# Low halves made on chip, a sixth pair, one power per norm and paced loads of x in a hybrid layer kernel

## The chip, the core and the metric

The kernel runs on one core of a Trainium2 chip, as one launch. The metric is the device time of that launch in microseconds; several runs are taken and their median is compared. The profile is of one execution more, recorded by the hardware profiler. In it PE is the matmul engine (TensorE), PEld its weight load, DVE the vector engine, ACT the scalar engine, POOL is GpSimd and SP the engine that only issues transfers.

## What is computed

One layer over 2048 prompt tokens and 64 tokens of a separate sample, which carries its own convolution history and its own state. Cut to what matters:

```python
h = rms_norm(x, g_pre)
vA, bA, cA, zA, q, f, iv, zB, gA, gB = split(h @ w_in)            # ten blocks of 1024 columns
conv = causal_conv3(concat(conv_hist, cA * vA), conv_w)
yA = (silu(zA) * bA * conv) @ w_a_out                              # convolution path
fg = lb + (1 - lb) * sigmoid(f); logf = log(fg); kk = 1 - fg       # attention path, 8 heads of 128
for each chunk of 64 tokens, b = cumsum(logf), ref = b[middle]:
    att = tril((qq * exp(b - ref)) @ (kk * exp(ref - b)).T)
    o = att @ vv + (qq * exp(b)) @ S
    S = exp(b_last) * S + (kk * exp(b_last - b)).T @ vv
o = o * rsqrt(mean(o * o) + 1e-6) * g_onorm
yB = (o * silu(zB)) @ w_b_out
x = x + rms_norm((sigmoid(gA) * yA + sigmoid(gB) * yB) @ w_o, g_post)
x = x + (p @ w_ple_proj) * sigmoid(rms_norm(x, g_ple) @ w_ple_gate)
```

The sample goes through the same layer with its own history and state.

## The kernel before

**Blocks.** Prompt and sample are laid in one row of 2112 tokens, the sample at place 1408. It is worked off in three blocks of 768, 704 and 640 tokens (`plan`, from L47). Everything is kept with features on the 128 partitions and tokens along the free dimension. The first block has six pairs of 64-token chunks, the second five pairs of the prompt and the sample's lone 64-token chunk, the third five pairs.

**Large products.** A float32 product is made of three matmuls in fp32r: high weight by high input (L442), high weight by low input (L443), low weight by high input (L444). `sgroup` makes two output blocks of 128 features at once by a scheme of seven products in place of eight, over halves of the contraction and of the tokens: its weight blocks are `A11`, `S3`, `S1`, `S2`, `A12`, `A22`, `S4`, in this order; `A..` are weights as they are, `S..` are sums of them. Each product takes 4 x 3 matmuls. `in_turn` (L593 to L595) and `gemm` (L631 to L633) do the same for the later products.

**Weights.** In the first block `combined` loads four weight blocks, makes the sums, and `split_w` makes of each block a high half on ACT and a low half on DVE (both recorded at L226, in `split`); the low halves and the sums are stored to HBM through SP for the later blocks (L280, L331), where `used_later` says so. In the later blocks `kept_w` loads the block (L236), ACT casts the high half (L273) and SP loads the stored low half (L274). Weight tiles rotate: five raw ones, four high ones, four plus three low ones (`lo` and `s` by turns, `low_tile`).

**Order.** Path B of a block (`path_b`) goes over eight heads. A head takes two groups by `sgroup` (f with iv, then zB with q). After each of the seven products `hook()` runs one prepared step, so the small float32 matmuls of a head's attention (`head_attn`) are put between the products of the groups that follow. In a block that is not the first the steps of one head stand at fixed slots: 2 (first part's scores), 3 (second part's), 6 (updates of the state, all pairs), 8 (outputs), 11 (`turn_o`), 14 (`read_o`), 21 (`scale_o`); the sample's chunk, a part of its own, has steps at 4 (two transposes and scores), 5 (update), 7 (output) and 10 (transpose back). The keys, values and outputs of the pairs are turned from features to tokens without PE: DVE transposes in 32 x 32 blocks (L1054), POOL stores to HBM (`turned`, L1056) and loads back in another order (`in_rows`, L1061); the keys are then copied by POOL (L1066) to the tile that the state updates read (L1126). Path A (`path_a`) follows with sixteen groups of `sgroup` (vA with cA, zA with bA), then the products with `w_a_out`, `w_b_out`, `w_o`. In the second block `prepare_sums` makes on the side, in path A, the sums for `w_b_out` for the block that follows.

**Norms.** At a block's end `final_norm` is spread by hooks over the next block's gate products. `col_rstd` sums squares over features by transposes (L709), a reduction (L711), a scaling (L686) and a power on POOL (L689), once for each half of the block; `rms` puts the result on all partitions by transposes again (`spread`, L700). x is loaded for it on POOL's queue (L1423), four tiles of 128 features ahead.

Of the kernel before, what the change touches and what calls it, by code (L numbers as in the profile page):

```python
# [47 lines left out]
def plan():  # L48
# [3 lines left out]
    for size in SIZES:  # L52
# [8 lines left out]
        assert all(g["len"] == 2 * CH for g in groups[:npair])  # L61
        parts = [groups[i : min(i + 4, npair)] for i in range(0, npair, 4)] + [[g] for g in groups[npair:]]
        halves = [dict(t0=t0 + o, off=o, n=size // 2) for o in (0, size // 2)]
        out.append(dict(t0=t0, n=size, runs=runs, npair=npair, parts=parts, groups=groups, segs=halves, last=t0 + size == TOK))
# [29 lines left out]
def hybrid_step(  # L94
# [102 lines left out]
    lone = [const.tile([P, 1, P], F32, tag=f"lone{i}", name=f"lone{i}") for i in range(3)]  # L197

    def constants():
        for rows, odd, base in ((slice(0, P), 0, 0), (slice(0, CH), 1, -CH), (slice(CH, P), 1, CH)):  # L200
            tri = rt(P)
            G.memset(tri, 1.0)
            G.affine_select(
                out=tri, in_=tri, pattern=[[1, P]], compare_op=ALU.is_ge, fill=0.0, base=base, channel_multiplier=-1
            )
            V.tensor_copy(caus[odd][rows], tri[rows])
        V.memset(keep, 1.0)
        V.memset(keep.rearrange("p (c t) -> p c t", t=CH)[:, :, 0:1], 0.0)
        for t in atts + lone:
            V.memset(t, 0.0)  # L210
# [40 lines left out]
    def used_later(idx, part):  # L251
# [5 lines left out]
        if idx in (GB * 8 + KB - 1, IV * 8):  # L257
            return part != 0
        if W_B <= idx < W_O:
# [74 lines left out]
    def kept_w(i1, i2, name, anew=False, spread=False):  # L334

        keys = dict(A11=(i1, 0), A12=(i1, 1), A22=(i2, 1))
        if name in keys:
            return split_w(load_raw(w_blk[keys[name]]), None if anew else keys[name], spread)
# [346 lines left out]
    def rstd_of(ms_ap, out_ap, scale, start=0):  # L685
# [3 lines left out]
        powers[:] = [G.tensor_tensor(out_ap, out_ap, mhalf[start : start + shape[0], :].to_broadcast(shape), ALU.pow).ins]  # L689
        return scaled  # L690

    def cols_tile(n):
        return small.tile([P, (n + P - 1) // P], F32, tag="cols", name=nm("cols"))
# [9 lines left out]
    def col_rstd(acc, n):  # L703

        pc = ps_attn()
        cols = cols_tile(n)
        with placed():
            for i, o in tiles_of(n):
                T.transpose(pc[:, i * P : i * P + P], acc[:, o : o + P], ident)  # L709
        count = cols.shape[1]  # L710
        V.tensor_reduce(cols, pc[:, : count * P].rearrange("p (i c) -> p i c", c=P), axis=mybir.AxisListType.X, op=ALU.add)  # L711
        rstd_of(cols, cols, 1.0 / D)
        return cols

    def rms(acc, out, segs, hasten=False):


        cols = [col_rstd(acc[:, cols_of(sg)], sg["n"]) for sg in segs]
# [217 lines left out]
    def head_prep(bl, hc, hd, first, hs, before):  # L936
        n, npair = bl["n"], bl["npair"]
        nch, np1 = n // CH, npair * P
        sf, vt = rt(), rt()

        def sink_f(c, h, x, y):
# [9 lines left out]
            into(half(vt, h)[:, n1:], x[:, n1:], None if y is None else y[:, n1:])  # L951
# [5 lines left out]
        lg, b, eq, qx = rt(), rt(), rt(), rt()  # L957
        wrote = [turned("tv", vt, qx, npair)]
# [8 lines left out]
        ka, kb, qe, z = hf(npair * CH), rt(), rt(), rt()  # L967

        def scaled(after):
# [17 lines left out]
            more = npair - 2 * SWAP  # L987
            for lo, hi, to in (
                (0, SWAP, ka3[:, more + 1 :: 2, :]),
                (SWAP, 2 * SWAP, ka3[:, more : npair - 1 : 2, :]),  # L990
                (2 * SWAP, npair, ka3[:, :more, :]),
            ):
                own = slice(2 * lo, 2 * hi, 2)
                V.tensor_tensor(to, chunks(sf)[:, own, :], chunks(lg)[:, own, :], ALU.mult)
                scale = f2[:, lo:hi].unsqueeze(2).to_broadcast([P, hi - lo, CH])
                place = slice(2 * lo + (hi <= SWAP), 2 * hi, 2)
                V.tensor_tensor(chunks(kb)[:, place, :], to, scale, ALU.mult)
# [3 lines left out]
            if not first:  # L1001
                wrote.append(turned("tk", kb, b, npair))
            if nch % 2:
                end = slice(nch - 1, nch)
                V.tensor_tensor(chunks(kb)[:, end, :], chunks(sf)[:, end, :], chunks(lg)[:, end, :], ALU.mult)
# [28 lines left out]
        with behind_all([*wrote, *powers]):  # L1034
            by_token = [in_rows("tv", npair)]
            if before is not None and not first:
                before["ot"] = in_rows("to", npair, before["on"])
            if not first:
                by_token.insert(0, in_rows("tk", npair))
        return dict(  # L1040
            eq=eq, f=f, ka=ka, kb=kb, qe=qe, qx=qx, vt=vt, z=z, by_token=by_token, on=None,
            npair=npair, more=npair - 2 * SWAP, first=first, last=bl["last"], carry=None,
# [26 lines left out]
    def head_attn(ip, gs, d, hd):  # L1069
# [3 lines left out]
        nt, ln = len(gs), gs[0]["len"]  # L1073
        o0, n = gs[0]["off"], nt * ln
        qe, z, att = d["qe"], d["z"], atts[ip]
        single = ln < P
        assert (nt == 2 * SWAP) == (o0 == 0)
        rows = slice(P - ln, P)

        def tile3(i=None):  # L1080
            if single and i is not None:
                return lone[i]
            if nt == 1:
                return small.tile([P, 1, P], F32, tag="one", name=nm("one"), bufs=5)
            return cols3(rt(nt * P), nt)

        def cols(t, g):
            end = g["off"] + ln
# [4 lines left out]
        ready = [] if single else [t[:, o0 // P : o0 // P + nt] for t in d["by_token"]]  # L1093
        for q, src in enumerate((d["kb"], d["vt"])[: 2 - len(ready)]):
            turn_ = ps_attn()
            with placed():
                for i, g in enumerate(gs):
                    T.transpose(turn_[:, i * P : i * P + P], cols(src, g), ident)
            ready.insert(q, tile3(q))
            A.copy(ready[q][rows], cols3(turn_, nt)[rows])  # L1100
        kt, v = ready
        p_a = ps_attn()
        with placed():
            for i, g in enumerate(gs):
                o = g["off"]
                shared = nt == 2 * SWAP
                if not single and (i < SWAP or not shared):
# [4 lines left out]
                T.matmul(p_a[:, i * P + CH : i * P + P], cols(d["kb"], g), qe[:, o + ln - CH : o + ln], start=True, stop=True)  # L1112
        pa3 = cols3(p_a, nt)

        if single:
            V.copy_predicated(att[CH:, :nt, CH:], caus[0][CH:, CH:].unsqueeze(1).to_broadcast([CH, nt, CH]), pa3[CH:, :, CH:])
        else:
            for swapped, lo, hi in ((1, 0, SWAP), (0, SWAP, nt)) if nt == 2 * SWAP else ((0, 0, nt),):
                mask = caus[swapped].unsqueeze(1).to_broadcast([P, hi - lo, P])
                V.copy_predicated(att[:, lo:hi], mask, pa3[:, lo:hi])  # L1120
# [8 lines left out]
        sample = gs[0]["sample"]  # L1129
        if sample:  # L1130
            cur = small.tile([P, P], F32, tag="s0", name=nm("s0"), bufs=1)
            G.dma_start(cur, s0[hd])
        else:
            cur = states[hd] if d["carry"] is None else d["carry"]
        for i, g in enumerate(gs):
            u = p_u[:, i * P : i * P + P]
            c = (g["off"] + ln) // CH - 1
# [7 lines left out]
        if g["end"]:  # L1145
# [6 lines left out]
            if sample:  # L1152
# [5 lines left out]
        else:  # L1158
            d["carry"] = cur
# [9 lines left out]
        if not single:  # L1169
            d["on"] = rt(d["npair"] * P) if d["on"] is None else d["on"]  # L1170
            on = cols3(d["on"][:, o0:], nt)
        else:
            on = tile3(2)
        ms = small.tile([P, 4], F32, tag="ms", name=nm("ms"))
        po3 = cols3(p_o, nt)
        if d["first"]:
            for i in range(nt):
                A.activation(on[rows, i, :], po3[rows, i, :], AF.Square, accum_out=ms[rows, i : i + 1])
        else:
            A.activation(on[rows], po3[rows], AF.Square)  # L1180
            V.tensor_reduce(ms[rows, :nt], on[rows], axis=mybir.AxisListType.X, op=ALU.add)
        rstd_of(ms[rows, :nt], ms[rows, :nt], 1.0 / P, P - ln)
# [605 lines left out]
```

## Time and profile before

| | |
|---|---|
| median of 3 runs | 2545.3 us (2542.03 to 2548.34) |
| the profiled execution | 2544.89 us, of which the span 2543.2 us |
| DVE, ACT, POOL busy | 71%, 59%, 18% of the span |
| granted TensorE clock | 1.000 |
| 16 DMA engines | 67.0% of their time on SP's queue, 21.3% on POOL's; 781.01 MB |

PE is busy 99% of the time. A page with such a figure is read by what PE executes and by the few places where it stands: its instructions in order of time, and the view of waits cut down to PE. A float32 matmul appears as two records (x2), a transpose as one; a large product's matmul as one. "Mean ns" of a matmul is from its start to its modelled end and overlaps the next one, so the price of one is read from start to start.

### The profile page before, as it was taken

How to read it: one execution, taken by the hardware profiler on the slowest of the kernel's cores; microseconds unless marked ns; L12 is line 12 of the kernel's file. 1: busy time of each engine (PE TensorE's matmuls, PEld its weight loads, DVE VectorE, ACT ScalarE, POOL GpSimd, SP SyncE). 2: the span in 40 equal slices, each digit the busy share in tenths (PEclk: the TensorE clock that was granted, in tenths of full speed). 3: DMA queues.
4: the chain of work that ended last, by engine and by line, in shares of the span. 5: the costliest groups of instructions: out<-in, count | busy, mean ns of one | idle time of the engine just before them, and what ended most of it. 6: DMA issues, size and time to landing. Idle time of an engine off the chain costs nothing.

```text
span 2543.2 us, 46984 instructions
## 1 busy us (share of the span) xinstructions
PE 2524.2 (99%) x16022; PEld 2511.2 (99%) x16022; DVE 1796.8 (71%) x3533; ACT 1499.3 (59%) x2940; POOL 462.7 (18%) x809
## 2 busy tenths in 40 slices
PE   9999999999999999999999999999999999999998
PEld 9999999999999999999999999999999999999998
DVE  7889888889868775467774557988347755336967
ACT  6766676554453764466655556567456665446674
POOL 2012121221022022122221221102212221001011
PEclk9999999999999999999999999999999999999999
DMA  8789888999797888988889998989999999999985
GB/s 331 246 291 340 305 297 304 349 354 328 258 345 250 274 288 306 309 286 299 294 298 308 357 380 307 327 289 308 333 306 317 319 337 322 298 299 327 334 270 195
DMA packets 371937, 781.01 MB, mean 307 GB/s; under 512 B 45990, under 2 KB 50912, under 8 KB 371696
## 3 DMA queue, kind: packets, MB, share of 16 engines
q1 hardware_dynamic: 321840, 582.95, 67.0%
q0 software_dynamic: 49856, 195.04, 21.3%
q8 instruction: 126, 2.06, 0.3%
q14 instruction: 115, 0.94, 0.1%
HBM read 562.57 MB, written 215.24 MB: 306 GB/s over the span
## 4 chain that ended last, share of the span: by engine, by line
PE 89%; DMA 4%; issue 3%; DVE 2%; ACT 0%; POOL 0%; SPq 0%; DVEq 0%; POOLq 0%; ACTq 0%
PE pg L442 19%; PE pg L444 19%; PE pg L443 19%; PE pg L593 5%; PE pg L594 5%; PE pg L595 5%; PE pg L632 3%; PE pg L633 3%; PE pg L631 3%; PE pa L1126 1%; PE pa L1166 1%; DMA lo<-low 1%; PE pa L1168 1%; PE pa L1112 1%; DMA s<-low 1%
## 5 line engine op out<-in xcount | busy, mean ns | idle before, releaser
L442 PE MATMUL pg<-r,hi 128*128 128x320 f32 (+2 forms) x3304 | 1078.7, 326 | 0.1
L443 PE MATMUL pg<-r,hi 128*128 128x320 f32 (+2 forms) x3304 | 1067.8, 323 | 0.0
L444 PE MATMUL pg<-r,lo 128*128 128x384 f32 (+2 forms) x2368 | 772.5, 326 | 1.7 <-DMA lo<-low 1.5
L273 ACT CAST hi<-raw 128x512 fp32r<-128x512 f32 x726 | 447.2, 619 | 486.3 <-PE pg L443 188.1
L442 PEld LDWEIGHTS pg<-r,hi 128*128 128x128 f32 x3304 | 621.6, 188 | 0.8 <-ACT hi L226 0.4
L443 PEld LDWEIGHTS pg<-r,hi 128*128 128x128 f32 x3304 | 621.4, 188 | 0.0
L444 PEld LDWEIGHTS pg<-r,lo 128*128 128x128 f32 x2368 | 444.6, 188 | 2.8 <-DMA lo<-low 2.1
L444 PE MATMUL pg<-r,s 128*128 128x320 f32 (+1 forms) x936 | 295.8, 316 | 2.0 <-DMA s<-low 2.0
L594 PE MATMUL pg<-r,hi 128*128 128x320 f32 (+2 forms) x864 | 277.5, 322 | 0.0
L593 PE MATMUL pg<-r,hi 128*128 128x320 f32 (+2 forms) x864 | 274.9, 322 | 0.2 <-ACT r L226 0.2
L226 ACT CAST hi<-raw 128x512 fp32r<-128x512 f32 x252 | 155.4, 621 | 151.5 <-PE pg L443 41.3
L226 DVE TENSOR_TENSOR r<-r,r 128x320 fp32r<-128x320 f32 (+7 forms) x350 | 206.4, 609 | 43.9 <-ACT r L226 42.9
L226 ACT CAST r<-r 128x320 fp32r<-128x320 f32 (+7 forms) x350 | 183.3, 557 | 43.9 <-DVE r L390 9.3
L226 DVE TENSOR_TENSOR lo<-raw,hi 128x512 fp32r<-128x512 f32 x231 | 157.7, 687 | 71.8 <-ACT hi L226 67.8
L595 PE MATMUL pg<-r,lo 128*128 128x352 f32 (+2 forms) x564 | 180.8, 321 | 0.4 <-DMA lo<-low 0.4
L444 PEld LDWEIGHTS pg<-r,s 128*128 128x128 f32 x936 | 176.0, 188 | 2.6 <-DMA s<-low 2.6
L226 ACT CAST hi<-s 128x512 fp32r<-128x512 f32 x160 | 98.9, 620 | 130.1 <-PE pg L443 106.1
L632 PE MATMUL pg<-r,hi 128*128 128x384 f32 (+2 forms) x512 | 167.5, 328 | 0.2 <-DVE r L226 0.2
L631 PE MATMUL pg<-r,hi 128*128 128x384 f32 (+2 forms) x512 | 166.0, 328 | 0.5 <-ACT hi L226 0.3
L594 PEld LDWEIGHTS pg<-r,hi 128*128 128x128 f32 x864 | 162.1, 188 | 1.2 <-DVE r L226 0.8
L593 PEld LDWEIGHTS pg<-r,hi 128*128 128x128 f32 x864 | 161.3, 188 | 1.6 <-ACT r L226 1.2
L456 ACT COPY hf<-pg 128x352 f32<-128x352 f32 (+2 forms) x354 | 157.4, 447 | 1.2 <-PE pg L444 0.8
(393 smaller groups left out, 4134.9 us busy)
## 6 DMA issues: line engine op xcount, KB each, us to landing
raw<-w_blk SPq DMA_DIRECT2D x578, 256.0 KB, 4.5
raw<-S SPq DMA_DIRECT2D x440, 256.0 KB, 4.6
lo<-low SPq DMA_DIRECT2D x421, 256.0 KB, 4.4
s<-low SPq DMA_DIRECT2D x305, 256.0 KB, 4.5
low<-lo SPq DMA_DIRECT2D x275, 256.0 KB, 4.2
S<-s SPq DMA_DIRECT2D x156, 256.0 KB, 4.0
low<-r POOLq DMA_DIRECT2D x50, 256.0 KB, 5.9
r<-w_blk POOLq DMA_DIRECT2D x48, 256.0 KB, 7.3
```

What stands on the lines that cost most here:

```text
L226: return A.copy(hi, src).ins, V.tensor_tensor(lo, src, hi.bitcast(F32), ALU.subtract).ins
L273: A.copy(hi, raw)
L442: add(hi[:, k, :], xhi, start=start and k == 0, stop=False)
L443: add(hi[:, k, :], xlo, start=False, stop=False)
L444: last[0] = add(lo[:, k, :], xhi, start=False, stop=k == KH - 1).ins
L456: copied = A.copy(got[n], ps[bank])
L593: add(hi[:, k, :], xhi, start=start and k == 0, stop=False)
L594: add(hi[:, k, :], xlo, start=False, stop=False)
L595: last[0] = add(lo[:, k, :], xhi, start=False, stop=k == KH - 1).ins
L631: T.matmul(ps, hi[:, k % 4, :], xhi[:, c], start=k == ks[0], stop=False)
L632: T.matmul(ps, hi[:, k % 4, :], xlo[:, c], start=False, stop=False)
L633: last[0] = T.matmul(ps, lo[:, k % 4, :], xhi[:, c], start=False, stop=k == ks[-1]).ins
```

## The change

1. **Low halves.** In path A of the second and third block the low halves of `A12` and `A22` of the four weights vA, bA, cA, zA are made by DVE from the raw tile, as in the first block, in place of the load; the first block does not store them.
2. **Sixth pair.** The sample's chunk becomes the second half of a sixth pair, whose first half has zero values and a copy of the chunk's keys. It shares the part of the fifth pair: its keys, values and outputs go through the same transposes on DVE and the same way through HBM (now 768 columns wide in place of 640), its scores come out of the fifth pair's first matmul, its update and output stand in that part's steps. The steps at slots 4, 5, 7 and 10 go.
3. **One power.** `col_rstd` takes both halves of a block, and makes one scaling and one power of all columns. In the plan of hooks the spreading of a block's first norm comes one hook later; five idle hooks between the norms become four.
4. **x one by one.** In the first two blocks the four loads ahead become one at each of the four steps that sum squares, and each load of x is held behind the last matmul issued before it (`paced`).
5. `prepare_sums` in the second block's path A takes its steps at groups' turns 0, 1, 3, 5, 7 in place of 3 to 7.

```diff
@@ used_later
+        if idx < QQ * 8:
+            return part != 1
@@ kept_w
-            return split_w(load_raw(w_blk[keys[name]]), None if anew else keys[name], spread)
+            return split_w(load_raw(w_blk[keys[name]]), None if anew else keys[name], spread or keys[name][0] < QQ * 8 and keys[name][1] == 1)
@@ col_rstd
+        count = len(tiles_of(n))
+        cols = small.tile([P, 2 * count], F32, tag="cols", name=nm("cols"))[:, : len(accs) * count]
+        outs = [cols[:, q : q + count] for q in range(0, len(accs) * count, count)]
+        for acc, out in zip(accs, outs):
+            pc = ps_attn()
...
+            V.tensor_reduce(out, pc[:, : count * P].rearrange("p (i c) -> p i c", c=P), axis=mybir.AxisListType.X, op=ALU.add)
         rstd_of(cols, cols, 1.0 / D)
-        return cols
+        return outs
@@ head_prep
+        odd_end = turn > npair
+        sf, vt = rt(), rt(turn * P)
+        if odd_end:
+            V.memset(vt[:, n - CH : n], 0.0)
...
+            if odd_end:
+                V.tensor_copy(chunks(kb)[:, nch - 1 : nch + 1, :], ka3[:, more - 1 : more, :].to_broadcast([P, 2, CH]))
...
-                wrote.append(turned("tk", kb, b, npair))
-            if nch % 2:
-                end = slice(nch - 1, nch)
-                V.tensor_tensor(chunks(kb)[:, end, :], chunks(sf)[:, end, :], chunks(lg)[:, end, :], ALU.mult)
+                wrote.append(turned("tk", kb, staged_k, turn))
@@ head_attn
+                if mixed:
+                    if i == 0:
+                        c = o // CH
+                        to = p_a[:, : 2 * 3 * CH].rearrange("p (g c) -> p g c", c=3 * CH)[:, :, :CH]
+                        T.matmul(to, d["ka"][:, :P], chunks(qe)[:, c : c + 3 : 2, :], start=True, stop=True)
...
+        if mixed:
+            V.copy_predicated(att[CH:, nt - 1, CH:], caus[0][CH:, CH:], pa3[CH:, nt - 1, CH:])
...
-        yield
-        p_t = ps_attn()
-        with placed():
-            for i in range(nt):
-                T.transpose(p_t[:, i * P : i * P + P], on[:, i, :], ident)
-        c = slice(o0, o0 + n)
-        V.tensor_tensor(z[:, c], p_t[:, P - ln : P - ln + n], z[:, c], ALU.mult)
@@ path_b
-                pairs, one = attn[:2], attn[2:]
-                for slot, steps in enumerate((pairs[:1], pairs[1:], one, one, pairs, one, pairs, (), one)):
+                for slot, steps in enumerate((attn[:1], attn[1:], (), (), attn, (), attn)):
@@ final_norm
-                G.dma_start(xks[j][:, c], x_fm[j * P : (j + 1) * P, segs[0]["t0"] : segs[0]["t0"] + n])
-
-        for _ in range(2 if bl["last"] else 4):
+                load = G.dma_start(xks[j][:, c], x_fm[j * P : (j + 1) * P, segs[0]["t0"] : segs[0]["t0"] + n])
+                if not bl["last"]:
+                    paced(load)
+
+        if kept is None:
             fetch()
-        if kept is not None:
+            fetch()
+        else:
             for j in range(KB):
                 sum_squares(j, xo[j], acc, width[0])
                 if j % 2:
+                    fetch()
                     yield
@@ side
-                if j >= 3:
+                if j in (0, 1, 3, 5, 7):
                     next(sums_, None)
@@ the plan of the first two blocks' norms
-            spread_out((norm, (1, 1, 1, 1, 0, 0, 1, 0, 1) + (0, 1) * KB + (0, 0, 0, 0, 0, 1, 0, 1) + (0, 1) * KB))
+            spread_out((norm, (1, 1, 1, 1, 0, 0, 1, 0, 0, 1) + (0, 1) * KB + (0, 0, 0, 0, 1, 0, 1) + (0, 1) * KB))
```

157 lines of the change are left out of this document (74 added, 83 removed).

## The prediction

> **What bounds the kernel now.** I read the page's head and chain first, then the view of waits for PE alone (total, times, longest), then PE's instructions around each wait.
>
> ```profile
> span 2543.2 us, 46984 instructions
> ...
> PE 2524.2 (99%) x16022; PEld 2511.2 (99%) x16022; DVE 1796.8 (71%) x3533; ACT 1499.3 (59%) x2940; POOL 462.7 (18%) x809
> ...
> PE 89%; DMA 4%; issue 3%; DVE 2%; ACT 0%; POOL 0%; SPq 0%; DVEq 0%; POOLq 0%; ACTq 0%
> ```
>
> ```profile
> PE pa L700 <- POOL cols L689: 2.9, 5, 0.8
> PE pg L444 <- DMA s<-low: 2.0, 2, 1.1
> PE pg L444 <- DMA lo<-low: 1.5, 2, 0.8
> ...
> PE pa L1126 <- POOL r L1066: 1.1, 2, 0.8
> ```
>
> PE sets the end: it stands for 2543.2 - 2524.2 = 19 us in all. So the change can gain in two ways only: by matmuls that PE no longer executes, and by those few waits. The kinds shown are the ones that it can reach, 7.5 us together. Work saved on another engine, or a transfer saved where PE didn't wait, counts nothing.
>
> **Matmuls removed.** In each of the second block's eight heads the lone chunk's steps at slots 4 and 10 go. Here they are (start, duration), the score step in one head and the transpose back in another:
>
> ```profile
> 1194.14 0.33 PE L443 MATMUL pg<-r,hi 128*128 128x352 f32 x1
> 1194.30 0.32 PE L444 MATMUL pg<-r,lo 128*128 128x352 f32 x1
> 1194.46 0.38 PE L1098 MATMUL pa<-ident,r 128*128 128x128 f32 x2
> 1194.68 0.33 PE L1112 MATMUL pa<-r,r 128*128 128x64 f32 x2
> 1194.82 0.41 PE L442 MATMUL pg<-r,hi 128*128 128x352 f32 x1
> 1195.07 0.32 PE L443 MATMUL pg<-r,hi 128*128 128x352 f32 x1
> ```
>
> ```profile
> 1110.11 0.33 PE L444 MATMUL pg<-r,s 128*128 128x352 f32 x1
> 1110.28 0.27 PE L1193 MATMUL pa<-ident,lone 128*128 128x128 f32 x1
> ...
> 1110.55 0.32 PE L443 MATMUL pg<-r,hi 128*128 128x352 f32 x1
> ```
>
> A plain step is 0.16 us (1194.14 to 1194.30). From 1194.30 to 1195.07 lie two plain steps and the lone work: 0.77 - 0.32 = 0.45 us for two transposes and the scores. From 1110.11 to 1110.55, two steps again: 0.44 - 0.32 = 0.12 us. The update (one float32 matmul) and the output (two) stay and only move into the pair's steps. Gain: 8 x 0.57 = 4.6 us. Against it, the pair's first score matmul becomes 128 wide:
>
> ```profile
> L1111 PE MATMUL pa<-r,hf 128*128 128x128 f32 x32 | 6.6, 286 | 0.0
> ...
> L1111 PE MATMUL pa<-r,hf 128*128 128x64 f32 x16 | 2.6, 246 | 0.0
> ```
>
> That is at most 0.04 us longer a record, two records a head, 0.6 us; it can also be nothing, since weight loads pace such short ones. I take 0.2, so 4.4 us.
>
> **Waits that go.** Path A of the second block, two of them (PE's idle time in the bracket); then the second norm's spreading and POOL's power; then POOL's burst of x:
>
> ```profile
> 1449.94 0.43 PE L444 MATMUL pg<-r,lo 128*128 128x352 f32 x1 [0.79 <-DMA lo<-low]
> ...
> 1484.27 0.43 PE L444 MATMUL pg<-r,s 128*128 128x352 f32 x1 [1.12 <-DMA s<-low]
> ```
>
> ```profile
> 463.00:690.00 227.00, 226.76 (x1304) 226.00 (x1303) 194.79 (x335) 116.03 (x239) 46.74 (x76) 1.00 0.92 324
> 1332.00:1542.00 210.00, 208.08 (x1301) 207.38 (x1301) 111.67 (x221) 112.64 (x226) 48.68 (x107) 1.00 0.97 346
> ```
>
> The second fence is the view of windows (PE, PEld, DVE, ACT, POOL busy, clock, DMA share, GB/s) for path A of the first and the second block. In the second the DMA engines are full, 0.97. Counted in products from their group's start, the wait at 1484 is for `A22`, whose load the change removes: 1.1 us, sure. That at 1449 is for `S1`, which is still loaded; but 2 of 14 weight transfers of each group are gone, and the side work that filled POOL's queue there (sums at turn 4) is moved off that turn. Between 0 and 0.8; I take 0.7.
>
> ```profile
> 1728.93 0.54 PE L700 MATMUL pa<-ident,cols 128*128 128x128 f32 x3 [0.63 <-POOL cols L689]
> ...
> 1730.41 0.54 PE L700 MATMUL pa<-ident,cols 128*128 128x128 f32 x3 [0.20 <-POOL cols L689]
> ```
>
> ```profile
> 1697.77 1.60 POOL L1423 DMA_DIRECT2D r<-x_fm  x3 [8.29 <-PE pg L595]
> ...
> 1729.47 0.88 POOL L689 TENSOR_TENSOR cols<-cols,mhalf 128x3 f32<-128x3 f32 x1
> ```
>
> ```profile
> PE pg L444 <- DMA s<-low: 0.9, 1, 0.9
> ```
>
> Each norm's two spreadings stand behind two powers. One power ends where now the second ends or earlier (1729.47 + 0.88 = 1730.35), and the spreading comes one product later, some 12 matmuls. In this norm PE loses 0.63 + 0.20 and the restart; I put 1.0 us on it and the same on the first block's, 2.0 us, between 0 and 2.2. What is late next: each later step of that norm by one hook, with one idle hook fewer before the second norm; if that is too few, it costs again what was gained, 2.0. The last wait (view of waits, 1700 to 1712) comes when three x loads, and a fourth behind them, start at 1697.77 in front of it. Spread over four steps they leave the DMA engines free: 0.9 us, between 0 and 0.9; I take 0.8. Behind a paced load POOL's queue holds the gates' stores and the norm's power; the matmul it waits for was issued before its own hook, so they move by a product at most.
>
> **What is added.** First, DVE makes 64 low halves (16 groups x 2 x 2 blocks):
>
> ```profile
> L226 DVE TENSOR_TENSOR lo<-raw,hi 128x512 fp32r<-128x512 f32 x47 | 32.3, 687 | 4.1 <-ACT hi L226 1.8 <-DMA low<-lo 1.5 <-issue 0.7
> ```
>
> ```profile
> PE pg L444 <- DVE lo L226: 0.2, 1, 0.2
> ```
>
> 64 x 0.69 = 44 us, half of it in the second block's path A, where DVE is busy 111.67 of 210 us. Path A of the first block does all its low halves this way with DVE at 194.79 of 227, and PE waits there 0.2 us (both rows from that window). By the order of instructions each subtraction stands behind the previous group's last sums, and PE needs it at the fifth and sixth product, so there are some three products (36 x 0.16 = 5.8 us) of cover. I take 0.3, between 0 and 1. If the cover is gone, PE stands at each of 64 places.
>
> Second, the way of the keys to the tokens grows by a fifth in width. It sets off PE's update at slot 6:
>
> ```profile
> 1150.47 0.54 POOL L1056 DMA_DIRECT2D tk<-r  x1 [3.51 <-DMA to<-r]
> ...
> 1156.32 0.75 POOL L1061 DMA_DIRECT2D r<-tk  x1 [3.79 <-DMA tk<-r]
> 1163.01 0.71 POOL L1066 COPY r<-r 128x640 f32<-128x640 f32 x1 [5.95 <-DMA r<-tk]
> ...
> 1264.75 0.72 POOL L1066 COPY r<-r 128x640 f32<-128x640 f32 x1 [7.26 <-DMA r<-tk]
> ```
>
> ```profile
> 1165.61 1.16 PE L1126 MATMUL pa<-r,r 128*128 128x128 f32 x9
> ...
> 1265.79 1.27 PE L1126 MATMUL pa<-r,r 128*128 128x128 f32 x10
> ```
>
> The copy ends 1.89 us ahead of PE in the one head (1165.61 - 1163.72) and 0.32 in the other, the tightest of the eight; most have about 2. The third block has no lone chunk, and there PE waited twice (the L1126 row above). Now PE comes 0.45 us earlier by the score step, and 0.22 by the update that leaves slot 5 (two records of 0.11): 0.67. The store and the reload took 1163.01 - 1150.47 = 12.5 us for 640 columns; 768 cost between 0, if latency rules, and a fifth more, 2.5; I take 0.4. The copy adds 0.14 (a fifth of 0.71). DVE's part:
>
> ```profile
> 1141.31 0.29 DVE L1188 TENSOR_TENSOR lone<-pa,ms 64x128 f32<-64x128 f32 x1 [0.76 <-POOL ms L689]
> ...
> 1144.72 1.35 DVE L1054 STREAM_TRANSPOSE r<-r 128x640 f32<-128x640 f32 x1
> ```
>
> It loses the lone chunk's scaling with its wait, 1.05, and gains a fifth of 1.35, 0.27, on each of two transposes and some 0.3 for the keys' copy (128 columns, as in the row of L1188): about even. So the slack shrinks by 1.2: one head waits 0.9, the rest don't. I take 1.0 us; the upper end, 0.67 + 0.14 + 2.5 = 3.3 in every head, is 3.0 + 7 x 1.4 = about 13. The Trainium skill, "DMA: Bandwidth & Descriptors", section "Anatomy of one DMA — SWDGE (gpsimd) path", fits a POOL-issued transfer by 2.0 us plus its bytes at 436 GB/s: an estimate of 0.15 us for 64 KB, 0.3 for both, and the term would be 0.9 us. The level of the fit doesn't hold here, where each leg takes about 6 us in place of 2.8; its slope no run here shows yet. The same skill, "SBUF — State Buffer", section "SBUF: two separate sides", says that a DVE instruction with two SBUF inputs and a GpSimd instruction that reads SBUF lock each other out; the added subtractions are of that kind, but they lie in path A, away from these copies.
>
> The 32 stores dropped in the first block count nothing: PE doesn't wait for a transfer there. The lone chunk's ACT copies and POOL powers lie beside PE's products.
>
> **Sum.** 4.4 + 1.1 + 0.7 + 2.0 + 0.8 = 9.0 gained, 0.3 + 1.0 lost: 7.7, and with a few tenths for DVE's and POOL's lighter load in the heads 8. The profiled execution took 2544.9 (span 2543.2 and 1.7 around it), 0.4 under the median of the runs shown: 2544.9 - 8 = 2537.
>
> **Rivals.**
> - Waits move, not vanish. DMA at 0.92 to 0.97 means that a late transfer shows up elsewhere; then only the matmuls and `A22` count: 4.4 + 1.1 - 1.3 = 4.2, 2540.7. For it: the two late `lo` and `s` loads are scattered. Against: the burst of side work and of x are what went before them. Chance 0.14.
> - The keys' way takes the place of the lone steps: PE waits at slot 6 in each head. With store and reload longer by 1.9 us in place of 0.4 the slack shrinks by 2.7: 2.4 + 7 x 0.8 = 8.0, less the 1.0 counted: 2544. At the upper end it is 13 - 1: 2549. For it: slack 0.32, and the third block's two waits. Against: most heads have 2 us. Chance 0.10.
> - Slower: the subtraction for `A12` or `A22` is late at PE in path A of both blocks, because DVE, in order, stands before it for ACT's cast or for POOL's history columns. At 0.4 us a place, 64 x 0.4 = 26 us: 2537 + 26 = 2563. It makes the kernel slower from 0.25 us a place on (16 us), that is when 5.8 us of cover are used up. Against: the first block's row, 0.2 us. Chance 0.11.
>
> **How the numbers follow.** A measurement of this kernel tells about 0.3% from no change, 7.6 us, so 2537.7 is the border below and 2552.9 the one above. The forecast, chance 0.65, lies just beyond the lower one; its own range, 2532 to 2540, lies on both sides of it, and I count 0.57 of the 0.65 as faster. Slower: 0.10 of the third rival and 0.02 of the second. Within 0.3%: the rest, 0.31. The range 2532 to 2546 takes in the first rival, most of the second and every gain at its upper bound with 2 to 3 us for other transfers; left out is the third rival and what lies below.
>
> **What would show it.** Right: L1098 and L1193 gone from the second block and PE's busy time down by about 4.5; no wait for `s` in its path A; L700's waits in the first two norms under 0.3 together; the L1126 wait for POOL's copy at one or two heads of the second block. Wrong: waits of L444 for DVE's low halves in path A, or L1126 waiting in most heads of the second block.

## The result, and the profile after

The change made the kernel slower: 2554.51 us (median of six runs, 2550.9 to 2561.22) against 2545.09 us (2542.03 to 2548.34), a ratio of 1.0039 with a 95% interval of 1.0024 to 1.0054, that is +9.4 us. The prediction, 2537 us and a range of 2532 to 2546, was wrong. The profiled execution took 2554.89 us; its mean granted clock was 0.997 where before it was 1.000.

First the page's head of the changed kernel, then its view of waits for PE (total, times, longest). Line numbers are those of the changed kernel: the large matmuls are at L443 to L445, the spreading at L698, the norm's sums over features at L710, the heads' outputs at L1172 and L1174, the state updates on DVE at L1149.

```profile
span 2553.2 us, 46693 instructions
...
PE 2527.2 (99%) x15982; PEld 2514.8 (98%) x15982; DVE 1837.4 (72%) x3581; ACT 1498.1 (59%) x2916; POOL 455.0 (18%) x797
```

```profile
PE pa L1174 <- DVE r L1149: 3.8, 1, 3.8
PE pa L710 <- DVE r L733: 3.8, 3, 3.3
PE pg L443 <- ACT hi L225: 2.2, 1, 2.2
...
PE pa L698 <- POOL cols L690: 1.5, 2, 0.8
...
PE pa L1172 <- DVE r L1149: 0.8, 1, 0.8
```

The 40 records that were to go are gone (16022 to 15982, five in each of eight heads), and so are the waits for `s`. But PE now stands for 26 us in place of 19, and the largest waits are new in kind: for DVE's state update in the last head, and for DVE's and ACT's work in the two norms. PE's busy time even rose, by 3 us, with 40 records fewer. The view of windows tells why (PE, PEld, DVE, ACT, POOL busy, granted clock, DMA share, GB/s): behind these waits the granted clock falls, to 0.50 at the lowest.

```profile
897.00:901.00 4.00, 3.60 (x16) 3.60 (x17) 3.26 (x8) 3.59 (x6) 0.49 (x1) 0.63 0.69 198
...
1342.00:1345.00 3.00, 2.41 (x10) 2.11 (x10) 2.83 (x6) 2.89 (x7) 0.00 (x0) 0.50 0.00 0
1345.00:1348.50 3.50, 3.24 (x13) 3.25 (x14) 3.50 (x11) 0.43 (x2) 0.91 (x2) 0.50 0.68 173
...
1730.00:1739.00 9.00, 6.09 (x28) 5.17 (x27) 6.54 (x11) 8.23 (x15) 0.00 (x0) 0.74 0.81 281
```

**The last head's outputs, at 1330 to 1348 (part 5).** These are the timelines of the changed kernel: POOL, then DVE, then PE (start, duration, engine and line; in the bracket the engine's idle time and what ended it).

```profile
1329.00 0.82 POOL L1073 COPY r<-r 128x768 f32<-128x768 f32 x1 [7.59 <-DMA r<-tk]
1329.78 2.16 POOL L380 DMA_DIRECT2D r<-w_blk  x4
```

```profile
1336.56 2.87 DVE L391 TENSOR_TENSOR r<-r,r 128x512 f32<-128x512 f32 x4 [7.75 <-DMA r<-w_blk]
...
1341.51 0.34 DVE L1149 SCALAR_TENSOR_TENSOR r<-state,qc,pa 128x128 f32<-128x128 f32 x1
```

```profile
1332.78 0.83 PE L1134 MATMUL pa<-r,r 128*128 128x128 f32 x6
...
1341.90 0.80 PE L1174 MATMUL pa<-r,r 128*128 128x128 f32 x2 [3.76 <-DVE r L1149]
1342.49 0.63 PE L1172 MATMUL pa<-r,att 128*128 128x128 f32 x2
1342.92 0.64 PE L1174 MATMUL pa<-r,r 128*128 128x128 f32 x2
```

With the side work at turn 0 POOL loads four weight blocks at 1329.78, right behind the last head's copy of the keys. The four additions of these blocks (L391) stand in DVE's queue ahead of the state updates. DVE works in order: it idles 7.75 us for the load, then adds for 2.87 us, and the first state update, whose inputs PE had finished by 1333.6 (1332.78 + 0.83, L1134), runs at 1341.51. In the kernel before it ran without such a wait:

```profile
1333.89 0.34 DVE L1143 SCALAR_TENSOR_TENSOR r<-state,qc,pa 128x128 f32<-128x128 f32 x1
```

The outputs need the states one after the other, and PE stands 3.76 and then 0.85 us. Behind it two records of a 128-wide matmul take 0.43 us (1342.49 to 1342.92) in place of 0.22.

**The norms (part 4).** Timelines of the changed kernel again: POOL, SP's issues, ACT, DVE and PE around the first norm.

```profile
882.79 2.12 POOL L1422 DMA_DIRECT2D r<-x_fm  x4 [27.20 <-PE pg L445]
...
883.66 0.37 SPq L235 DMA_DIRECT2D raw<-S  x1
...
887.42 0.33 SPq L235 DMA_DIRECT2D raw<-w_blk  x1
892.96 0.33 SPq L235 DMA_DIRECT2D raw<-S  x1
...
892.31 0.62 ACT L274 CAST hi<-raw 128x512 fp32r<-128x512 f32 x1 [3.43 <-DMA raw<-S]
...
893.71 0.96 DVE L733 TENSOR_TENSOR r<-r,r 128x768 f32<-128x768 f32 x1 [3.14 <-ACT r L732]
...
897.40 0.96 PE L710 MATMUL pa<-ident,r 128*128 128x128 f32 x6 [3.31 <-DVE r L733]
...
898.45 0.49 PE L444 MATMUL pg<-r,hi 128*128 128x352 f32 x1
898.75 0.49 PE L443 MATMUL pg<-r,hi 128*128 128x352 f32 x1
```

The four x loads are not "one by one": they go out within 2.12 us. Each is held behind the last matmul issued before it; the first gate group issues its first four products ahead of any hook, so these four steps have the same matmul before them and all four loads are released by it (27.20 <-PE pg L445). The block of weights that SP issues at 883.66 lands 8.6 us later; ACT's cast at 892.31 waits for it 3.43 us, the norm's squares (ACT L732) are queued behind the cast, the sums (DVE L733) behind the squares, and PE, in order too, waits 3.31 us for the sums. SP issues nothing from 887.42 to 892.96. This is the view of SP's weight loads by their line (L235, 882 to 889), the time from issue to landing, in the changed kernel and then in the one with parts 4 and 5 undone (below):

```profile
DMA to landing us min/median/max: 2.8/8.7/9.2
```

```profile
DMA to landing us min/median/max: 2.7/4.5/5.1
```

The same loads take twice as long behind the bunch. In the second norm the same row stands at 1721.12, and PE waits 2.2 us for ACT's `hi`. Behind these waits, too, a step takes longer: 0.30 us (898.45 to 898.75) in place of 0.16.

### The profile page after: what moved, and what is told of

Its sections match the earlier page's. It is cut to its first block, busy times and chain, and to the rows that moved or that the text cites. A ratio compares the mean times of both kernels' runs of the same rounds, so it can differ in the third digit from the quotient of the medians.

```text
span 2553.2 us, 46693 instructions
## 1 busy us (share of the span) xinstructions
PE 2527.2 (99%) x15982; PEld 2514.8 (98%) x15982; DVE 1837.4 (72%) x3581; ACT 1498.1 (59%) x2916; POOL 455.0 (18%) x797
## 4 chain that ended last, share of the span: by engine, by line
PE 73%; DVE 3%; DMA 3%; issue 2%; ACT 1%; POOL 0%; SPq 0%; DVEq 0%; ACTq 0%; POOLq 0%
PE pg L445 15%; PE pg L443 15%; PE pg L444 15%; PE pg L595 5%; PE pg L594 5%; PE pg L596 5%; PE pg L634 3%; PE pg L633 3%; PE pg L632 3%; DMA raw<-S 1%; PE pa L1134 1%; PE pa L1172 1%; PE pa L1174 1%; PE pa L1121 1%; DMA S<-r 0%
## 5 line engine op out<-in xcount | busy, mean ns | idle before, releaser
L443 PE MATMUL pg<-r,hi 128*128 128x320 f32 (+2 forms) x3304 | 1078.0, 326 | 3.2 <-ACT hi L225 2.2
L445 PE MATMUL pg<-r,lo 128*128 128x384 f32 (+2 forms) x2368 | 773.4, 327 | 2.1 <-DMA lo<-low 1.5
L443 PEld LDWEIGHTS pg<-r,hi 128*128 128x128 f32 x3304 | 623.4, 189 | 3.9 <-ACT hi L225 2.5
L445 PEld LDWEIGHTS pg<-r,lo 128*128 128x128 f32 x2368 | 445.4, 188 | 3.3 <-DMA lo<-low 1.8
L445 PE MATMUL pg<-r,s 128*128 128x320 f32 (+1 forms) x936 | 297.0, 317 | 0.7 <-DVE s L225 0.7
L225 DVE TENSOR_TENSOR lo<-raw,hi 128x512 fp32r<-128x512 f32 x263 | 180.3, 690 | 77.9 <-ACT hi L225 74.3
L225 ACT CAST r<-r 128x320 fp32r<-128x320 f32 (+7 forms) x350 | 183.6, 558 | 44.2 <-DVE r L391 10.2
L445 PEld LDWEIGHTS pg<-r,s 128*128 128x128 f32 x936 | 176.6, 189 | 1.0 <-DVE s L225 1.0
```

The costliest lines, as they stand in the source:

```text
L225: return A.copy(hi, src).ins, V.tensor_tensor(lo, src, hi.bitcast(F32), ALU.subtract).ins
L443: add(hi[:, k, :], xhi, start=start and k == 0, stop=False)
L445: last[0] = add(lo[:, k, :], xhi, start=False, stop=k == KH - 1).ins
```

## The experiments

"Undone" means that the changed kernel got this part back as it was before; "alone" means that the kernel before got this part only. Each is compared with runs of the kernel before on the same chip. The ratio is estimated from all runs and is not the quotient of the two medians. By its intervals a price in microseconds is uncertain by 2 to 4, and one that compares two rows by more; where parts are priced below, the differences of the medians are used.

| kernel | median, us | before | difference | ratio (95%) |
|---|---|---|---|---|
| changed kernel | 2554.51 | 2545.09 | +9.4 | 1.0039 (1.0024 to 1.0054) |
| 4 undone | 2546.09 | 2543.95 | +2.1 | 1.0017 (1.0008 to 1.0026) |
| 5 undone | 2543.25 | 2543.95 | -0.7 | 0.9994 (0.9986 to 1.0003) |
| 4 and 5 undone | 2533.96 | 2543.95 | -10.0 | 0.9959 (0.9947 to 0.9972) |
| 2 alone | 2538.95 | 2543.95 | -5.0 | 0.9984 (0.9975 to 0.9993) |
| 4 alone | 2549.59 | 2543.25 | +6.3 | 1.0026 (1.0017 to 1.0035) |
| 5 alone | 2559.24 | 2543.25 | +16.0 | 1.0063 (1.0048 to 1.0078) |
| 5 undone, x loads held behind three products | 2534.59 | 2543.25 | -8.7 | 0.9965 (0.9952 to 0.9978) |
| 4 undone, turns 1, 2, 3, 5, 7 | 2541.0 | 2543.25 | -2.3 | 0.9990 (0.9980 to 1.0000) |
| 1, 4, 5 undone | 2538.43 | 2543.41 | -5.0 | 0.9980 (0.9968 to 0.9991) |
| 3, 4, 5 undone | 2534.84 | 2543.41 | -8.6 | 0.9964 (0.9951 to 0.9976) |
| 1 alone | 2540.57 | 2543.41 | -2.8 | 0.9987 (0.9978 to 0.9995) |
| 4 undone, additions held behind the head | 2538.77 | 2542.69 | -3.9 | 0.9984 (0.9975 to 0.9993) |

**Part 4 undone.** The theory was that the bunched x loads make the norms' waits; the rival that the DMA engines are simply fuller.

```diff
-                if not bl["last"]:
-                    paced(load)
...
-        if kept is None:
-            fetch()
+        for _ in range(2 if bl["last"] else 4):
             fetch()
-        else:
+        if kept is not None:
...
-                    fetch()
```

> The changed kernel with part 4 alone undone (four loads of x ahead, not held). Theory: the four steps are all released by the end of the first gate group, whose first four products are issued before any hook, so the four held loads start at one moment (882.79 and 1721.12 us) together with the weights of the next products; a sum's load lands 3.4 us late, ACT stands for it, and PE after it. Undone, PE's wait for the first norm's transposes after the first block (3.3 us) and for the high half after the second (2.2 us) go, with the half-speed matmuls behind them: about 8 us less, 2546 to 2548. Rival (the one power and the later hook delay the norm): the waits stay, 2553 to 2556.

The norms' waits are gone (L710 for DVE: 0.2 us in place of 3.8) and the last head's stay (PE waits 4.4 and 0.9 us at L1174 and L1172). Against the changed kernel this one gains 7 us and is still 2.1 us slower than before: another part costs as well.

**Part 5 undone.**

```diff
-                if j in (0, 1, 3, 5, 7):
+                if j >= 3:
```

> The changed kernel with part 5 alone undone (the sums for the next block take their steps at turns 3 to 7 again). Theory: at turn 0 of the second block's path A the side work's first additions stand in DVE's queue behind loads issued only 7 us earlier, and the last head's state updates stand behind them; PE waits 3.8 and 0.8 us for the state and then runs its matmuls at half speed for some 3 us. Undone, the wait of PE for DVE's state row in the second block and the slow matmuls after it are gone: about 7 us less than the changed kernel, 2547 to 2548. Rival (the longer way of the sixth pair delays the state): PE still waits there, within 2 us of 2554.

The wait for the state update is gone, the norms' waits stay (L710 5.2 us in three, `hi` 1.3). The time is that of the kernel before, 4 us below what was expected.

**Both undone.**

Both diffs above.

> The changed kernel with parts 4 and 5 undone; low halves on chip, the sixth pair and the one power stay. Theory: both stalls gone and the forecast's gains stand: 2537 to 2540, faster than before by 0.2 to 0.3%. Rival (sixth pair or low halves cost): 2546 or more.

2533.96 us: 10.0 us faster than before, 3 us below what was expected. This is the lowest median of all, and the version to keep; the intervals of three others overlap its own. The page's head of this kernel, then its view of waits for PE:

```profile
span 2532.3 us, 46692 instructions
...
PE 2517.0 (99%) x15982; PEld 2505.6 (99%) x15982; DVE 1836.2 (73%) x3581; ACT 1495.3 (59%) x2916; POOL 453.0 (18%) x797
```

```profile
PE pa L698 <- POOL cols L690: 2.8, 4, 0.8
...
PE pa L1134 <- POOL r L1073: 0.5, 1, 0.5
```

So parts 1 to 3 bring 10.0 us, and 4 and 5 take 19.4. The profiled executions differ by 20.9 us of span, in two nearly equal shares. PE stands for 26.0 us in the changed kernel and for 15.3 here, 10.7 more; the waits named above are 3.8 + 0.8 + 3.8 + 2.2 = 10.6. And for the same 15982 records PE is busy 10.2 us longer (2527.2 against 2517.0). The lower clock makes most of this: a mean of 0.997 over 2553 us, where this kernel has 1.000, is some 8 us of full clock.

**Part 4 alone, part 5 alone.** The two diffs above the other way round, on the kernel before.

> The kernel before with part 4 alone (x held, one load a step). Theory: the four loads again start at one moment at the end of the first gate group, with no other part of the change there: PE waits for the first norm's transposes or for a high half by 2 to 4 us in each of two norms and runs some 3 us at a lower clock behind: 8 to 10 us over the kernel before. Rival (the burst hurts only together with the six-column power and the later hook): within 3 us of before.

> The kernel before with part 5 alone (turns 0, 1, 3, 5, 7). Theory: the last head's state updates again stand behind additions that wait for loads: a wait of PE of 3 to 5 us at the start of the second block's path A and a lower clock behind it, 8 to 11 us over the kernel before (the two waits of path A for low halves may move too). Rival (it needs the sixth pair's later update): within 3 us of before.

Part 4 costs 6.3 us alone, some less than was expected, by the same wait (L709 for DVE's sums, 5.4 us in three). Part 5 costs 16.0, more than was expected and than in company (12.1: "4 undone" against "both undone"). Timelines of DVE and PE with part 5 alone (numbers of the kernel before: L390 are the additions, L1120 the masking of the scores, L1112 the products with the masked scores):

```profile
1336.51 1.42 DVE L390 TENSOR_TENSOR r<-r,r 128x512 f32<-128x512 f32 x2 [10.66 <-DMA r<-w_blk]
...
1338.28 0.29 DVE L1120 COPY_PREDICATED att<-caus,pa 128x128 f32<-128x128 int32 x1
```

```profile
1338.62 0.69 PE L1112 MATMUL pa<-r,r 128*128 128x64 f32 x2 [9.11 <-DVE att L1120]
```

Here two of the additions were placed even earlier, ahead of the mask of the last head's scores, and PE stood 9.11 us. A second wait followed, 3.30 us at 1382.03 for DVE's `hf` (L462), behind an addition for whose load DVE had idled 11.19 us. The mechanism is the same one; which step of the head is caught, and so the price, depends on where the additions fall in DVE's order.

**Held, but really one by one.** Is it the holding back that costs, or that four come at once? Part 5 undone, and three held loads at three hooks behind the sums, each with a product of its own before it:

```diff
                 if j % 2:
-                    fetch()
                     yield
+            for _ in range(3):
+                fetch()
+                yield
...
-            spread_out((norm, (1, 1, 1, 1, 0, 0, 1, 0, 0, 1) + (0, 1) * KB + (0, 0, 0, 0, 1, 0, 1) + (0, 1) * KB))
+            spread_out((norm, (1, 1, 1, 1, 1, 1, 2, 0, 0, 1) + (0, 1) * KB + (0, 0, 0, 0, 1, 0, 1) + (0, 1) * KB))
```

> The changed kernel with part 5 undone and part 4 in another form: three loads of x held, one at each of the hooks behind the fifth, sixth and seventh product, which have matmuls of their own between them. Theory (the burst is the cost, not the holding): like the kernel with parts 4 and 5 undone, 2532 to 2537. Rival (a held load in POOL's queue, or x coming late, is the cost): 2541 to 2545, as with part 5 alone undone.

POOL's timeline of this kernel:

```profile
883.23 0.54 POOL L1422 DMA_DIRECT2D r<-x_fm  x1 [29.13 <-PE pg L445]
885.41 0.54 POOL L1422 DMA_DIRECT2D r<-x_fm  x1 [1.64 <-ACT r L732]
887.10 0.54 POOL L1422 DMA_DIRECT2D r<-x_fm  x1 [1.15 <-PE pg L445]
```

The loads start at 883 as in the changed kernel, but some 2 us apart (the second is released by ACT's squares, not by a matmul); the weight load that took 8.6 us takes 4.4, and L710 waits 0.7 us in all. It gains 8 us against "5 undone" and equals "both undone". So the loads may be late and held without a cost. That it is their spacing alone isn't shown, since two more things differ: there are three and not four, and SP's stream runs earlier here, so that the weight load in question is issued at 882.17, ahead of the first of them. Loads of weights are still slowed: in the window of the view above (882 to 889) the median is 5.9 us and the longest 7.2, between the 4.5 and 5.1 without loads of x and the 8.7 and 9.2 behind the bunch. Loads made truly one by one are no faster than the plain ones of before, though: 0.9965 and 0.9959, with intervals that overlap.

**Side turns one later.** If the clash with the last head is the whole cost of part 5, turns 1, 2, 3, 5, 7 should be free of it. Part 4 is undone.

```diff
-                if j in (0, 1, 3, 5, 7):
+                if j in (1, 2, 3, 5, 7):
```

> The changed kernel with part 4 undone and the side work's turns at 1, 2, 3, 5, 7 in place of 0, 1, 3, 5, 7. Theory (the first additions collide with the last head's steps, which end in turns 0 and 1): the loads come a turn later, the additions behind the state updates: PE's 4.4 and 0.9 us of wait gone, 2533 to 2537. Rival (two turns of side work in a row are too much for DMA or DVE in any place): 2541 to 2546.

A miss: 2541.0. The state wait is gone and another is there, in a later group of path A. Timelines of POOL, DVE and PE of this kernel:

```profile
1404.70 0.54 POOL L380 DMA_DIRECT2D r<-w_blk  x1 [1.01 <-DMA S<-r]
```

```profile
1412.56 0.69 DVE L391 TENSOR_TENSOR r<-r,r 128x512 f32<-128x512 f32 x1 [7.52 <-DMA r<-w_blk]
1413.16 0.68 DVE L225 TENSOR_TENSOR s<-raw,hi 128x512 fp32r<-128x512 f32 x1
```

```profile
1413.90 0.66 PE L445 MATMUL pg<-r,s 128*128 128x352 f32 x1 [3.57 <-DVE s L225]
```

The last of the four blocks is issued at 1404.70, behind a store on POOL; DVE idles 7.52 us for it, and the low half of `A22`, which part 1 now makes on DVE, stands behind the addition. So the early turns clash not only with the last head: in this group they clash with part 1.

**Part 5 kept, the additions held behind the head.** This tells the two costs of part 5 apart: the place in DVE's queue, and the transfers at that place. Part 4 is undone; the additions wait for the last head's transposes of outputs, so that they can't stand before its state updates.

```diff
+    turned_o = []
...
-        V.transpose(blocks4, src[:, :n].rearrange("p (g b j) -> p g j b", b=32, j=4))
+        done = V.transpose(blocks4, src[:, :n].rearrange("p (g b j) -> p g j b", b=32, j=4)).ins
+        if kind == "to":
+            turned_o[:] = [done]
...
-            V.tensor_tensor(out, x, y, op)
+            with behind_all(() if pieces or shared else turned_o):
+                V.tensor_tensor(out, x, y, op)
```

> The changed kernel with part 4 undone, part 5 kept (turns 0, 1, 3, 5, 7), and the side work's additions held behind DVE's last transposes of the last head's outputs. Loads and turns are as in the kernel with part 4 alone undone (2546); only the place of the additions in DVE's queue differs. Theory (DVE, in order, stands before the state updates for loads just issued): PE's waits for the state at the start of the second block's path A gone, 2533 to 2537. Rival (the loads and stores of the early turns themselves, or the sixth pair's later update, are the cost): 2543 to 2547.

2538.77 us: 6 us of the 12.1 are back (+2.1 to -3.9), and the waits for the state are gone. So the place in DVE's queue is a cause, but not the whole of the price: 2533 to 2537 was missed. View of windows of path A, this kernel and then "4 and 5 undone":

```profile
1322.00:1532.00 210.00, 207.16 (x1294) 206.17 (x1294) 125.20 (x244) 111.69 (x224) 49.46 (x109) 1.00 0.90 310
```

```profile
1332.00:1542.00 210.00, 210.00 (x1313) 209.93 (x1313) 131.59 (x253) 114.41 (x233) 48.65 (x104) 1.00 0.90 312
```

In path A 2.8 us of PE's time are still lost (210.00 - 207.16), 1.7 of them in one wait for a low half behind an addition, as in the kernel above but shorter; DVE's timeline of this one (L392 are its additions):

```profile
1410.20 0.69 DVE L392 TENSOR_TENSOR r<-r,r 128x512 f32<-128x512 f32 x1 [5.67 <-DMA r<-w_blk]
1410.82 0.68 DVE L225 TENSOR_TENSOR s<-raw,hi 128x512 fp32r<-128x512 f32 x1
```

The profiled executions of this kernel and of "both undone" differ by 4.8 us of span: 3.3 of standing (18.6 against 15.3), most of it in path A, and 1.5 of busy time, which no view here explains. By the medians, each against its own runs of before, the two are 6.1 apart; the intervals (0.9975 to 0.9993 and 0.9947 to 0.9972) don't tell 4.8 from 6.1.

**Parts 1 to 3 apart.** Part 2 alone, part 1 alone, 2 with 3, 1 with 2 (of part 3 the diff shows one line; `col_rstd` and the plan of hooks go back as well):

```diff
@@ 1 undone
         if idx < QQ * 8:
-            return part != 1
+            return True
...
-            return split_w(load_raw(w_blk[keys[name]]), None if anew else keys[name], spread or keys[name][0] < QQ * 8 and keys[name][1] == 1)
+            return split_w(load_raw(w_blk[keys[name]]), None if anew else keys[name], spread)
@@ 3 undone
-        cols = col_rstd([acc[:, cols_of(sg)] for sg in segs], segs[0]["n"])
+        cols = [col_rstd(acc[:, cols_of(sg)], sg["n"]) for sg in segs]
```

> The kernel before with the sixth pair alone. Theory: PE's 32 lone matmuls gone and no more wait than before, 2540 to 2541.5, with PE busy some 4.4 us less. Rival (the keys' longer way makes PE wait at slot 6 in each head): 2545 to 2550, with waits of the state update for POOL's copy in most heads of the second block.

> The kernel before with part 1 alone: 64 loads and 32 stores of low halves gone, 64 subtractions more on DVE. Forecast: the waits for low halves in the second block's path A gone, 1.8 us, less 0.3: 2542 where before is 2543.5. Rival (subtractions late at the fifth and sixth product): over 2545, with waits of PE for DVE's low halves in path A.

> The changed kernel with parts 1, 4 and 5 undone: the sixth pair and the one power alone. By the forecast the low halves on chip are worth 1.8 us (waits for low halves in the second block's path A) less 0.3: 2535.5 to 2537 here, against 2534.0 with them. Rival (DVE's 44 us of subtractions cost as much as they gain): 2534 or less.

> The changed kernel with parts 3, 4 and 5 undone: low halves and the sixth pair alone. By the forecast the one power with its later hook is worth 2.0 us: 2536 here, against 2534.0 with it. Rival (the trace of the kernel with both parts undone still shows one wait of 0.6 and one of 0.8 us for the power, which takes 1.37 us for six columns in place of 0.88 for three): worth under 1 us, 2533.5 to 2535.

The pair gives 5.0 us. The low halves give 2.8 alone, 3.6 on top of the pair (8.6 - 5.0) and 5.0 on top of parts 2 and 3 (10.0 - 5.0), each more than was expected. The window of path A with the low halves loaded as before ("1, 4, 5 undone"), and PE's waits in it:

```profile
1332.00:1542.00 210.00, 208.06 (x1298) 207.40 (x1297) 112.74 (x220) 112.87 (x229) 48.01 (x104) 1.00 0.97 346
```

```profile
PE pg L443 <- ACT hf L457: 1.6, 1, 1.6
PE pg L445 <- DMA s<-low: 0.3, 1, 0.3
```

With the halves made on chip PE stands nowhere in these 210 us (210.00 in the row above), the DMA share falls from 0.97 to 0.90, and DVE's 19 us more are hidden. But of the 1.9 us that PE stands here only 0.3 is for a low half. The 1.6 are for a copy by ACT, behind DVE's `hf`, and DVE had idled 7.73 us for the last head's outputs on their way back from HBM. With the DMA engines at 0.97 the late transfer is not always the same one. The one power gives nothing that can be told: 2534.84 without it and 2533.96 with it. The rows of the waits, first without and then with it ("both undone"; L701 is L698 there):

```profile
PE pa L701 <- POOL cols L690: 2.9, 5, 0.8
```

```profile
898.85 0.87 PE L698 MATMUL pa<-ident,cols 128*128 128x128 f32 x6 [0.60 <-POOL cols L690]
```

with POOL before it, in the same kernel:

```profile
896.87 0.54 POOL L866 DMA_DIRECT2D g__2709_11136<-r  x1 [29.66 <-ACT r L859]
897.43 1.37 POOL L690 TENSOR_TENSOR cols<-cols,mhalf 128x6 f32<-128x6 f32 x1
```

## Why the prediction was wrong

Two steps failed, the x loads (0.8 us gained) and the moved side work (a part of S1's 0.7), and together these two parts cost 19.4 us. Parts 1 to 3 brought 10.0 us where their terms add up to 6.9 (4.4 + 1.8 + 2.0 - 1.3), and of these the norms' 2.0 didn't come; that they gained more than was forecast is luck. In the profile of "both undone" PE's busy time fell by 7.2 us (2524.2 to 2517.0) and its standing by 3.7 (19.0 to 15.3); where the rest of the 7.2 comes from, beyond the matmuls removed, is open. The terms in turn:

- **Matmuls removed, 4.4.** Right in kind: 40 records went. With part 2 alone PE's busy time fell by 3.5 us (2524.2 to 2520.7) and the median by 5.0 (interval of the ratio: 1.8 to 6.4 us).
- **A22's and S1's waits, 1.8.** Right in sum: both are gone, and PE's 208.08 us in the window became 210.00 in "both undone". S1's wait went there with the side work back at turns 3 to 7, so moving it was not what took the wait away. The size agrees in part by luck: without part 1 PE stood 1.9 us again, but mostly for something else (above). In company the part is worth 3.6 to 5.0 in the medians; these differ by less than their intervals.
- **Norms' spreading, 2.0.** Failed, without weight for the result: waits of 2.9 us in five became 2.8 in four. In either view 1.5 of it lies at the end, in the last block's norms, so in the two norms that were meant 1.4 us in three stayed 1.4 in two. The six-column power takes 1.37 us, and it stands behind a gate's store on POOL; "one power ends where now the second ends or earlier" held only for a power that starts where the first one did.
- **DVE's low halves, 0.3; the keys' way, 1.0.** Right in kind: in "both undone" PE waits for no low half of DVE's in path A (0.7 us in the changed kernel), and once, 0.5 us, for the keys; the copy took 0.82 us where 0.85 was worked out. Without part 1 ("1, 4, 5 undone") PE waited at two heads, 1.8 us in all, so the slack is as thin as was said.
- **The x burst, 0.8 gained.** This step failed. "Spread over four steps they leave the DMA engines free" took the diff's word for it; and "the matmul it waits for was issued before its own hook" was written down without asking which matmul it is. It is the same for all four. The loads became a bunch as dense as before (2.12 us) and some 18 us later, where weights are just being loaded; they delayed the weights' loads (8.6 us for one that takes 4.3 in "both undone"), and by way of ACT and DVE the norms' sums. Price: 6.3 us alone, 9.3 in company ("5 undone" against "both undone").

The view of windows shows the move; the changed kernel, then "both undone":

```profile
865.00:875.00 10.00, 10.00 (x59) 10.00 (x59) 8.43 (x16) 5.35 (x10) 0.00 (x0) 1.00 0.68 205
...
887.00:892.00 5.00, 5.00 (x32) 5.00 (x32) 3.37 (x5) 1.88 (x3) 0.00 (x0) 1.00 0.99 371
```

```profile
865.00:875.00 10.00, 10.00 (x60) 10.00 (x59) 8.42 (x16) 5.34 (x10) 2.10 (x4) 1.00 0.93 317
...
887.00:892.00 5.00, 5.00 (x33) 5.00 (x33) 4.72 (x7) 5.00 (x9) 0.00 (x0) 1.00 0.93 345
```

The same four loads at 865 filled a stretch in which nothing was urgent. At 887 the DMA engines are full with them and the weights, and ACT is busy 1.88 us in place of 5.00, since it waits for a weight.

- **Part 5, counted as a gain inside S1's 0.7.** This is the other step that failed. "The side work that filled POOL's queue there (sums at turn 4) is moved off that turn" looked at the place that it left and not at the places where it went, turns 0 and 1, beside the last head's attention steps. There the additions, waiting 7.75 us for their loads, stood in DVE's queue before the state updates. Price: 12.1 us in company, 16.0 alone, 6 of the 12.1 by the additions' place before the last head's state updates.
- **The rivals.** The third, slower since "DVE, in order, stands before it", named the right engine and the right mechanism, but not the right place nor what DVE stands for: mostly the state updates were late, and behind the side work's loads, not behind ACT's cast. Where a subtraction was late (0.7 us in the changed kernel, 1.1 in "5 undone", 3.6 with the later turns), an addition of the side work stood before it. "Waits move, not vanish" holds in kind: at the last head they moved by the order of DVE's queue, in the norms by x loads beside weights, while path A's DMA share fell.
- **The price of a wait.** Every wait in the prediction was priced at its length. In the changed kernel, against "both undone", 10.7 us more of standing came with 10.2 us more of busy time for the same records.

## What to carry to other kernels

A hold "behind the last matmul" is only as fine as the matmuls between two holds: where several steps fall between the same two matmuls, all they hold is released together, so count the releasers and not the steps. When side work is moved, read every in-order queue at the place where it arrives: an addition that waits for a load blocks all that stands behind it on its engine, and moving it by one turn may only change what it blocks. And in a kernel that is bound by matmuls a stall of 2 to 4 us may cost more than its length, here about twice in sum, because the matmuls behind it ran at the lower clock.

## What the runs showed of the hardware

In the changed kernel the granted clock of TensorE fell to 0.50 in three places. In windows of 2 us it was 0.76, 0.50 and 0.88 from 897 to 903, behind a wait of 3.31 us. It was 0.95 over 1340 to 1342, 0.50 from 1342 to 1348 and 0.85 over 1348 to 1350, behind one of 3.76 with a second of 0.85. And it was 0.58 over 1734 to 1736, 0.50 to 1740 and 0.71 over 1740 to 1742, behind one of 2.22 with 0.45 and 0.24 close behind. Worked out from these windows, the clock was low for some 3.4, 6.8 and 6.8 us, and 8.5 us of full clock were lost. Single waits of 1.64 us ("1, 4, 5 undone") and 1.7 us ("additions held behind the head") left it at 1.00. Nine 352-wide steps at the lower clock took 2.64 us (898.45 to 901.09), 0.29 each in place of 0.16. The Trainium skill, "TensorE: Matmul & The Clock Gate", section "Part 1: The HAM clock gate (the "warmup" mystery)", says that the clock is halved after an idle window of about 3.4 us and comes back after a busy one. The waits of 3.31 and 3.76 us agree with this within 0.4 us, while the drop behind 2.22 us comes after less idle time than the page would have it, and the step grew 1.8 times (0.29 to 0.16), not quite twice.

A bunch of loads from one queue delayed those of another: with four loads of x issued on POOL's queue within 2.12 us, the weight loads that SP issued from 882 to 889 took 8.7 us in the median from issue to landing, and 4.5 where no x was loaded beside them.
